# Sums of exponentials of the second row moved to PSUM, with new transfer widths

## Chip, cores, metric

One core of one Trainium2 chip. The metric is the device time of one execution, in microseconds; a kernel is run several times, and fast runs are compared with fast runs. (A run more than 1.5% above the fastest of its kernel would count as slow.)

## The reference

```python
batch, num_classes = 256, 32000            # logits float32, labels int32, smoothing 0.1
log_probs = logits - max(logits)           # per row
log_probs = log_probs - log(sum(exp(log_probs)))
smooth_targets[i, :] = smoothing / num_classes      # at the label: + 1 - smoothing
return -sum(smooth_targets * log_probs, axis=-1)
```

So each row needs two sums over 32,000 columns, one of the logits and one of their exponentials, the logit at the label, and one logarithm (Ln). The input is 32.77 MB and is read once.

## The kernel before

Each of the 128 partitions holds two rows. The first row comes in three transfers, the second in eleven that get shorter. For every transfer VectorE (DVE) sums the logits and ScalarE (ACT) takes exponentials (the exponentials themselves go to a "junk" tile that nobody reads; only their sum counts); each instruction writes its sum with a second, small one that reads the engine's accumulator ("READ_ACCUMULATOR": 0.187 us a piece on ScalarE and 0.08 on VectorE where it writes SBUF, in the profile of before).

```python
WIDTHS = (
    (8000, 12480, 11520),
    (8192, 6336, 4608, 3392, 2496, 1920, 1472, 1152, 960, 768, 704),
)
TURN_MAX = 4608
...
turn = ctx.enter_context(tc.tile_pool(name="turn", bufs=2))
...
esum = small.tile([P, len(WIDTHS[-1])], FP32, name="esum", tag="esum")   # SBUF
...
def sum_exps(xt, w, out):
    if w > TURN_MAX:
        ja = junk.tile([P, max(WIDTHS[0])], BF16, name="ja", tag="ja")
    else:
        ja = turn.tile([P, TURN_MAX], BF16, name="jt", tag="jt")
    return nc.scalar.activation(out=ja[:, :w], in_=xt[:, :w], func=AF.Exp, accum_out=out)
...
elast = psum.tile([P, 1], FP32, name="elast", tag="elast")
pairs = [small.tile([P, 2], FP32, ...) for i in range(2)]                # SBUF
for t, w in enumerate(WIDTHS[r]):          # left = transfers still to come
    part = sum_logits(xt, w, xsum[:, t + 1 : t + 2] if left > 1 else pairs[1 - left][:, 0:1])
    if left == 0:    exps = sum_exps(xt, w, elast[:])
    elif left <= 2:  exps = sum_exps(xt, w, pairs[2 - left][:, 1:2])
    else:            exps = sum_exps(xt, w, esum[:, t : t + 1])
    ...
    # left == 2: reduce xsum and esum into done[0]; left == 1, 0: done[i+1] = done[i] + pairs[i]
...
nc.scalar.activation(out=lse[:], in_=elast[:], func=AF.Ln, bias=done[2][:, 1:2])
```

The softmax here doesn't subtract the row's maximum and nothing guards it: scores larger than these inputs give would overflow.

## Time and profile before

| | before |
|---|---|
| time, median of 3 runs | 84.26 us (84.2 to 84.3) |
| span of the profile | 82.4 us |
| ScalarE busy, VectorE busy | 70%, 45% |
| mean HBM rate over the span | 398 GB/s |
| last transfer lands (estimate in the prediction) | 78.53 us |
| Ln starts | 79.50 us |

How to read it: neither engine is busy all the time, the transfers are (DMA share 0.97 to 1.09 in each of five windows that cover 1 to 78 us). What can be gained lies between the last landing and Ln; the prediction shows the lines.

### The profile page before, as it was taken

What the parts mean: (1) busy time and instruction counts of PE and PEld (TensorE: products, weight loads), DVE (VectorE), ACT (ScalarE), POOL (GpSimd) and SP (SyncE); (2) the same over time, 40 slices, a digit from 0 to 9 for tenths busy, and PEclk for the clock granted to TensorE, in tenths of its full rate; (3) what the DMA queues carried; (4) which work ended last, traced back from release to release, by engine and by line L of the source; (5) the groups of instructions that cost most, each with busy time, mean ns of one, the idle gap of its engine ahead of it and who ended that gap; (6) DMA issues with size and microseconds to landing.
All of it is one profiled execution on the core that took longest, in us unless ns stands there. A gap on an engine that the chain in (4) does not pass through costs nothing.

```text
span 82.4 us, 227 instructions
## 1 busy us (share of the span) xinstructions
PE 6.9 (8%) x21; PEld 4.9 (6%) x21; DVE 36.9 (45%) x35; ACT 58.1 (70%) x31; POOL 9.7 (12%) x19
## 2 busy tenths in 40 slices
PE   0000000000000000000000000000100000999020
PEld 0000000000000000000000000000000000886000
DVE  0000002980000999300399606950695845757760
ACT  5000002999100999992399999999999999999960
POOL 3201640030100000000000004970000000000000
PEclk9999999999999999999999999999999999999995
DMA  6999999999998889988969969998999999999800
GB/s 131 387 428 420 419 591 388 388 388 436 630 484 358 358 358 402 671 358 358 461 302 509 509 267 517 455 394 376 429 429 430 421 428 425 420 420 411 348 0 0
DMA packets 2258, 32.77 MB, mean 398 GB/s; under 512 B 337, under 2 KB 338, under 8 KB 1106
## 3 DMA queue, kind: packets, MB, share of 16 engines
q1 hardware_dynamic: 2018, 30.71, 87.8%
q10 hardware_dynamic: 144, 2.06, 5.9%
q0 software_dynamic: 96, 0.00, 0.1%
HBM read 32.77 MB, written 0.00 MB: 398 GB/s over the span
## 4 chain that ended last, share of the span: by engine, by line
DMA 48%; ACT 47%; issue 1%; SPq 0%; PE 0%; DVE 0%; ACTq 0%
DMA wide<-in_logits_dram 48%; ACT ja L209 27%; ACT jt L209 19%; SPq L188 0%; PE lse_t L216 0%; DVE res L315 0%; ACT lse L310 0%; ACT lse L250 0%; ACTq L209 0%
## 5 line engine op out<-in xcount | busy, mean ns | idle before, releaser
L209 ACT ACTIVATE ja<-wide 128x8000 bf16<-128x8000 f32 (+4 forms) x5 | 39.8, 7958 | 20.7 <-DMA wide<-in_logits_dram 20.7
L194 DVE SCALAR_TENSOR_TENSOR jd<-wide 128x4000 f32<-128x4000 f32 (+11 forms) x12 | 34.4, 2870 | 38.9 <-DMA wide<-in_logits_dram 38.9
L209 ACT ACTIVATE jt<-wide 128x4608 bf16<-128x4608 f32 (+6 forms) x7 | 14.6, 2093 | 0.0
L301 PE MATMUL warm<-wide,ident 128*128 128x256 f32 x18 | 6.0, 508 | 11.6 <-DMA wide<-in_logits_dram 11.6
L236 POOL TENSOR_TENSOR acc<-acc,sums 128x2 f32<-128x2 f32 x1 | 4.1, 4127 | 12.6 <-ACT ja L209 12.6
L301 PEld LDWEIGHTS warm<-wide,ident 128*128 128x128 f32 x18 | 4.7, 267 | 12.8 <-DMA wide<-in_logits_dram 11.9
L216 PE MATMUL loss_t<-ident,loss 128*1 128x128 f32 x1 | 0.4, 373 | 58.1 <-POOL loss L252 58.1
L216 PEld LDWEIGHTS loss_t<-ident,loss 128*1 128x1 f32 x1 | 0.1, 79 | 58.1 <-POOL loss L252 58.1
L236 POOL TENSOR_TENSOR acc<-sums 128x2 f32<-128x2 f32 x1 | 0.2, 192 | 16.2 <-ACT ja L209 16.2
L132 POOL DMA_INDIRECT gat<-in_logits_dram,flat_idx x2 | 2.0, 994 | 0.7 <-POOL ident masks.py:199 0.4
L255 DVE COPY res<-loss_t 1x128 f32<-1x128 f32 x1 | 0.3, 280 | 3.8 <-PE loss_t L216 3.8
L99 ACT ACT_TABLE_LOAD x1 | 1.3, 1283 | 0.9 <-PEq L342 0.9
L209 ACT ACTIVATE jt<-tail 128x768 bf16<-128x768 f32 (+1 forms) x2 | 1.6, 800 | 0.0
L153 POOL TENSOR_SCALAR weighted<-gat 128x1 f32<-128x1 f32 x1 | 0.8, 812 | 6.4 <-DMA gat<-in_logits_dram,flat_idx 6.4
L209 ACT ACTIVATION_READ_ACCUMULATOR jt<-wide 128x1 f32 x7 | 1.3, 187 | 0.0
L194 DVE SCALAR_TENSOR_TENSOR jd<-tail 128x384 f32<-128x384 f32 (+1 forms) x2 | 1.1, 542 | 0.0
L194 DVE DVE_READ_ACCUMULATOR jd<-wide 128x1 f32 x12 | 1.0, 81 | 0.0
L209 ACT ACTIVATION_READ_ACCUMULATOR ja<-wide 128x1 f32 x5 | 0.9, 187 | 0.0
L112 POOL DMA_DIRECT2D lab<-in_labels_dram x1 | 0.8, 766 | 1.0 <-POOLq L342 1.0
L124 POOL TENSOR_TENSOR flat_idx<-rowoff,lab 128x2 int32<-128x2 int32 x1 | 0.2, 193 | 5.3 <-DMA lab<-in_labels_dram 5.3
L153 POOL TENSOR_SCALAR xsum<-gat 128x1 f32<-128x1 f32 x1 | 0.2, 208 | 2.9 <-DMA gat<-in_logits_dram,flat_idx 2.9
L216 PE MATMUL lin_t<-ident,done 128*1 128x128 f32 x1 | 0.3, 270 | 3.3 <-DVE done L294 3.3
(22 smaller groups left out, 4.3 us busy)
## 6 DMA issues: line engine op xcount, KB each, us to landing
wide<-in_logits_dram SPq DMA_DIRECT2D x1, 6240.0 KB, 26.0
wide<-in_logits_dram SPq DMA_DIRECT2D x1, 5760.0 KB, 39.2
wide<-in_logits_dram SPq DMA_DIRECT2D x1, 4096.0 KB, 29.2
wide<-in_logits_dram SPq DMA_DIRECT2D x1, 3168.0 KB, 19.9
wide<-in_logits_dram SPq DMA_DIRECT2D x1, 2304.0 KB, 25.0
wide<-in_logits_dram ACTq DMA_DIRECT2D x1, 2016.0 KB, 13.8
wide<-in_logits_dram SPq DMA_DIRECT2D x1, 1984.0 KB, 11.4
wide<-in_logits_dram SPq DMA_DIRECT2D x1, 1696.0 KB
```

The source lines that it names most:

```text
L99: nc.scalar.add_instruction(mybir.InstLoadActFuncSet(name=nc.get_next_instruction_name(), act_func_set_id=tbl, ins=[], outs=[],))
L112: nc.gpsimd.dma_start(out=lab[:], in_=labels.bitcast(I32).rearrange("(p f) -> p f", p=P))
L124: nc.gpsimd.tensor_tensor(out=flat_idx[:], in0=rowoff[:], in1=lab[:].rearrange("p (r two) -> p r two", two=2)[:, :, 0:1], op=ALU.add,)
L132: nc.gpsimd.indirect_dma_start(out=gat[:, r : r + 1], out_offset=None, in_=logits[:], in_offset=bass.IndirectOffsetOnAxis(ap=flat_idx[:, r ...
L153: nc.gpsimd.tensor_scalar(out=weighted[r], in0=gat[:, r : r + 1], scalar1=label_weight, scalar2=None, op0=ALU.mult,)
L194: return nc.vector.scalar_tensor_tensor(out=jd[:, :h], in0=xt[:, :h], scalar=1.0, in1=xt[:, h:w], op0=ALU.mult, op1=ALU.add, accum_out=out,)
L209: return nc.scalar.activation(out=ja[:, :w], in_=xt[:, :w], func=AF.Exp, accum_out=out)
L216: nc.tensor.transpose(out=row[:], in_=column, identity=ident[:])
L236: nc.gpsimd.tensor_tensor(out=acc[:], in0=total, in1=sums[:, :, t : t + 1], op=ALU.add)
L255: nc.vector.tensor_copy(out=res[:, :, 0:1], in_=loss_t[:])
L301: nc.tensor.matmul(warm[:], lhsT=ident[:], rhs=xt[:, i * WARM_COLS : (i + 1) * WARM_COLS], start=True, stop=True,)
```

## The change

The intent: in the profile of before ScalarE's one accumulator read to PSUM took 0.149 us, those to SBUF 0.187 us, so eight sums go to a PSUM tile (esum) and two to the PSUM tiles pair0 and pair1; with cheaper steps the widths can shrink towards a shorter last transfer (576 instead of 704 columns).

```diff
-    (8192, 6336, 4608, 3392, 2496, 1920, 1472, 1152, 960, 768, 704),
+    (8640, 6400, 4608, 3392, 2496, 1856, 1408, 1088, 832, 704, 576),
...
-    esum = small.tile([P, len(WIDTHS[-1])], FP32, name="esum", tag="esum")
+    esum = psum.tile([P, len(WIDTHS[-1]) - 3], FP32, name="esum", tag="esum")
...
-        small.tile([P, 2], FP32, name=f"pair{i}", tag=f"pair{i}") for i in range(2)
+        psum.tile([P, 2], FP32, name=f"pair{i}", tag=f"pair{i}") for i in range(2)
```

## The prediction

> **What bounds the kernel now.** I read the page first, then the chain of waits in order of time, then the timelines of ScalarE (ACT) and VectorE (DVE) near the end, then the windows of the last microseconds.
>
> The page's slices show the transfers busy to slice 37 and nothing after:
>
> ```profile
> ACT  5000002999100999992399999999999999999960
> DMA  6999999999998889988969969998999999999800
> ```
>
> The chain in order of time names transfers up to 40.46 us and ScalarE from there to the end:
>
> ```profile
> 1.29 39.17 DMA wide<-in_logits_dram
> ...
> 76.73 0.98 ACT jt L209 x2
> 77.71 0.01 issue
> 77.72 0.85 ACT jt L209 x2
> 78.57 0.07 issue
> 78.64 0.84 ACT jt L209 x2
> 79.47 0.02 issue
> 79.50 0.27 ACT lse L310
> ```
>
> That looks like a ScalarE bound, but the VectorE timeline corrects it. These rows are start, length, instruction, and in brackets the idle time before it with what ended it:
>
> ```profile
> 63.15 2.56 DVE L194 SCALAR_TENSOR_TENSOR jd<-wide 128x2304 f32<-128x2304 f32 x1 [1.01 <-DMA wide<-in_logits_dram]
> ...
> 76.78 0.66 DVE L194 SCALAR_TENSOR_TENSOR jd<-wide 128x480 f32<-128x480 f32 x1 [0.41 <-DMA wide<-in_logits_dram]
> ...
> 78.55 0.52 DVE L194 SCALAR_TENSOR_TENSOR jd<-tail 128x352 f32<-128x352 f32 x1
> 79.00 0.08 DVE L194 DVE_READ_ACCUMULATOR jd<-tail 128x1 f32 x1
> 79.19 0.16 DVE L294 TENSOR_TENSOR done<-done,pair 128x2 f32<-128x2 f32 x1
> ```
>
> VectorE waits for each transfer and starts at its landing; ScalarE starts the same transfer at most 0.12 us later (63.17 and 76.82 for these two). So the stream sets the pace and the widths were already shaped so that ScalarE finishes one transfer as the next lands. The starts of 4608 columns (63.15) and of 768 columns (77.69, also VectorE's) are 12,160 columns apart: 14.54 us / 12,160 = 1.196 ns a column, against 0.833 ns a column on ScalarE. In the windows, the DMA share is 0.97 in 77.5 to 78.0 us and 0.07 in the next half microsecond. The last landing, estimated, is 77.69 + 704 x 1.196 ns = 78.53 us. No split of the same bytes moves that, while the stream has no hole. **What can be won is only what lies between 78.53 and 79.50 us**, where Ln starts; from Ln on (transpose, add, output transfer) nothing changes.
>
> The ScalarE rows of the end:
>
> ```profile
> 77.81 0.83 ACT L209 ACTIVATE jt<-tail 128x768 bf16<-128x768 f32 x1
> 78.54 0.19 ACT L209 ACTIVATION_READ_ACCUMULATOR jt<-tail 128x1 f32 x1
> 78.64 0.77 ACT L209 ACTIVATE jt<-tail 128x704 bf16<-128x704 f32 x1
> 79.31 0.15 ACT L209 ACTIVATION_READ_ACCUMULATOR jt<-tail 128x1 f32 x1
> 79.50 0.26 ACT L310 ACTIVATE lse<-elast,done 128x1 f32<-128x1 f32 x1
> ```
>
> The read of the accumulator takes 0.187 us on average (the groups' mean) where it writes SBUF, and 0.149 us in the one case where its target, elast, is in PSUM. From the start of 768 columns to that of 704 it is 0.83 us, 0.64 of columns and 0.19 of fixed cost: 0.093 from ACTIVATE and 0.094 from the read.
>
> [...] 827 ns at 768 columns is 640 + 187, and the read starts 0.10 before the ACTIVATE's end. [...] The trace agrees for latency, 149 against 187 ns; it does not show whether the next instruction also starts earlier, since Ln had to wait for elast. [...]
>
> **The change, part by part.** *Ten of the second row's eleven sums go to PSUM* (eight in esum, two in the pairs; the last was there). If the overlap stays 93 ns, the read costs ScalarE 149 - 93 = 56 ns instead of 94, so a transfer costs 0.149 instead of 0.187 us beyond its columns. This is worth 0.38 us of ScalarE time over ten, but ScalarE waits for the stream, so most turns into idle time, not into an earlier end.
>
> *The widths.* Arrivals, counted back from 78.53 at 1.196 ns a column: 576 at 78.53, 704 at 77.84, 832 at 77.00, 1088 at 76.00, 1408 at 74.70, 1856 at 73.02, 2496 at 70.80, 3392 at 67.81, 4608 at 63.76, 6400 at 58.24, 8640 at 50.59. ScalarE takes each at its arrival + 0.04, or when free. From 2496, at 70.84: 70.84 + 2.080 + 0.149 = 73.07 (1856), + 1.547 + 0.149 = 74.77 (1408), + 1.322 = 76.09 (1088), + 1.056 = 77.15 (832), + 0.842 = 77.99 (704), + 0.736 = 78.73 (576). Then 0.480 + 0.093 to the last read, 79.30, and 0.19 to Ln as now: **79.49, against 79.50**. The last transfer is 128 columns (0.107 us) shorter but starts 0.09 later than the last one now, because the smaller steps leave ScalarE a small backlog. Without the PSUM saving the same sum from 3392 on with 0.187 gives a last start of 78.97 and Ln at 79.73.
>
> *The pairs in PSUM.* Column 0 of each is written by VectorE, column 1 by ScalarE for the transfer before. In SBUF these had nothing to do with each other. [...] I expect VectorE's sum of the last but one transfer to wait until ScalarE has finished the transfer before it, and likewise for the last. The path then is: ScalarE's 832 starts 77.15, its read ends at 77.15 + 0.693 + 0.093 + 0.149 = 78.09; VectorE starts the 704 at 78.12; its read 0.45 later as in the rows above (79.00 - 78.55), the add 0.19 later at 78.76, the next sum 0.18 later at 78.94; for 288 columns a side 0.45 - 64/960 = 0.38 to the read, 79.32, add at 79.51, end 79.67, and 0.05 to whoever waits (79.35 to TensorE's 79.40 now): **Ln at 79.72, 0.22 us later than now**. Without the wait, VectorE starts the 832 at 77.00, the two reductions cost 0.33 as now, 704 starts about 77.84, the last add ends at 79.39, and Ln is ScalarE's again at 79.49. Ln needs both engines, so the larger counts.
>
> **The rivals.** *Saving without wait*: Ln at 79.49, 84.25 us. For it: the program runs VectorE and ScalarE in near lockstep, and the wait might already be over. Against: before, VectorE's last sum starts at 78.55, before ScalarE's previous read has ended (78.73). *Saving and wait*: +0.22, 84.48 us; VectorE becomes the bound at the very end. *No saving in issue, only in latency*: +0.23 without the wait (84.5), +0.44 with it (84.7); for it speaks that the next ACTIVATE may be bound by issue, not by the end of the read. *Everything better than I count*: if the read to PSUM hides wholly, ScalarE takes each transfer at arrival, the last at 78.57, and Ln comes at 78.57 + 0.573 + 0.19 = 79.33, -0.17, 84.1 us. *The transfers move*: larger rows of 8640 columns, or a hole in the stream since the first buffer is awaited; nothing in the DMA slices speaks for it, as 8640 is issued after the same release as 8192.
>
> **Range and chances.** I give the saving 0.8 and a wait that binds 0.45, and so: saving alone 0.44 x -0.01, both 0.36 x 0.22, wait alone 0.09 x 0.44, neither 0.11 x 0.23; the sum is +0.14. The widths were chosen by someone who measured, which speaks for the lower side, so I shade it to +0.04: 84.3 us. The range takes in -0.26 (all hidden, and a little of the stream's spread: the three runs differ by 0.1) to +0.3 (both engines' costs). Two per cent is 1.69 us, more than the whole 0.97 us between last landing and Ln; faster by that is impossible unless the stream changes, slower needs a hole in it. Faster 0.01, within 0.98, slower 0.01.
>
> **What would show it.** The ten reads near 149 ns instead of 187, and the time from read start to next ACTIVATE 0.056 instead of 0.094: the saving. VectorE's starts on 832, 1088 and 1408 columns at about 77.00, 76.00, 74.70: the stream is unmoved. The wait: VectorE's rows for 352 and 288 columns starting just after ScalarE's reads, with idle time put down to ScalarE. ScalarE's last ACTIVATE at 78.7, and Ln after VectorE's last add or after the last read tells which engine ends it. I would be wrong if ScalarE shows gaps growing to the end (a larger saving), if the last landing is not near 78.5, or if VectorE's reads from PSUM take longer than the 156 to 161 ns of the reductions and adds now.

The forecast's sum: 0.44 x -0.01 + 0.36 x 0.22 + 0.09 x 0.44 + 0.11 x 0.23 = +0.14 us, shaded to +0.04, which on 84.25 us gives the 84.3. The constants are from the rows of before. ScalarE's 0.833 ns a column is (4027 - 774) ns / (4608 - 704) columns; the 93 ns of overlap are the read's 187 ns less 94 from its start to the next ACTIVATE (0.09 or 0.10 in the rows); 64/960 us is 64 columns at VectorE's rate, (6659 - 524) ns / (6240 - 352) columns = 1.042 ns. That no split moves the last landing was an estimate; after's 832 columns landed at 76.89 us where it gave 77.00.

## The result and the profile after

85.31 us median (85.12 to 85.45, 4 runs) against 84.25 us (4 runs): 1.06 us slower, ratio 1.0121, 95% interval 1.0103 to 1.0139. (Ratios and intervals are from fast runs alone; they are not quite the ratios of the medians quoted.) That is outside the predicted range of 84.0 to 84.6. The profiled run of after was the fastest of its four, 85.12 us with a span of 83.3 us, so its trace shows 0.9 of the 1.06 us.

The slices of after first:

```profile
ACT  5000003999001999990599998999999999999960
DMA  5999998899888899888996999999999999999300
```

The transfers still end in slice 37. In the windows the share of the DMA engines is 0.68 in 77.5 to 78.0 us and 0.01 in the next half microsecond, where before had 0.97 and 0.07: the stream is not what got longer. ScalarE's timeline of after (start us, length us, instruction), in the middle and at the end of the second row:

```profile
67.77 0.15 ACT L209 ACTIVATION_READ_ACCUMULATOR jt<-wide 128x1 f32 x1
67.96 3.03 ACT L209 ACTIVATE jt<-wide 128x3392 bf16<-128x3392 f32 x1
70.89 0.15 ACT L209 ACTIVATION_READ_ACCUMULATOR jt<-wide 128x1 f32 x1
71.08 2.29 ACT L209 ACTIVATE jt<-wide 128x2496 bf16<-128x2496 f32 x1
...
77.78 0.15 ACT L209 ACTIVATION_READ_ACCUMULATOR jt<-wide 128x1 f32 x1
77.83 0.89 ACT L209 ACTIVATE jt<-wide 128x832 bf16<-128x832 f32 x1
78.62 0.16 ACT L209 ACTIVATION_READ_ACCUMULATOR jt<-wide 128x1 f32 x1
78.67 0.79 ACT L209 ACTIVATE jt<-tail 128x704 bf16<-128x704 f32 x1
79.35 0.17 ACT L209 ACTIVATION_READ_ACCUMULATOR jt<-tail 128x1 f32 x1
79.40 0.69 ACT L209 ACTIVATE jt<-tail 128x576 bf16<-128x576 f32 x1
79.97 0.18 ACT L209 ACTIVATION_READ_ACCUMULATOR jt<-tail 128x1 f32 x1
80.36 0.26 ACT L310 ACTIVATE lse<-elast,done 128x1 f32<-128x1 f32 x1 [0.21 <-DVE done L294]
```

Two kinds of step are to be seen. The reads are short, as hoped: 0.15 us in the middle. But at 67.77 and 70.89 the next ACTIVATE comes **0.19 us** after the start of the read, when the read has ended; at 77.78, 78.62 and 79.35 it comes **0.05 us** after it. Before, it was 0.09 or 0.10 us between these steps. At one place before had 0.22 us: the read at 50.25 is followed by an ACTIVATE at 50.47, though its columns had landed by 50.22, where VectorE starts on them. In the compiled program that ACTIVATE waits for the one before it, as the junk tile of the long transfers has one buffer. So the price of such a wait stood in the trace of before. The last ACTIVATE starts at 79.40 instead of 78.64.

VectorE's timeline of after, near the end:

```profile
76.89 0.59 DVE L194 SCALAR_TENSOR_TENSOR jd<-wide 128x416 f32<-128x416 f32 x1 [0.28 <-DMA wide<-in_logits_dram]
...
77.97 0.17 DVE L289 TENSOR_REDUCE done<-esum 128x1 f32<-128x8 f32 x1 [0.47 <-ACT jt L209]
...
78.81 0.53 DVE L194 SCALAR_TENSOR_TENSOR jd<-tail 128x352 f32<-128x352 f32 x1 [0.60 <-ACT jt L209]
79.26 0.14 DVE L194 DVE_READ_ACCUMULATOR jd<-tail 128x1 f32 x1
...
80.11 0.16 DVE L294 TENSOR_TENSOR done<-done,pair 128x2 f32<-128x2 f32 x1
```

The 832 columns land at 76.89 us (predicted 77.00), so the stream is in place. VectorE then sits idle for ScalarE twice, which no row of before shows: for the sums in esum, and before the sum of the 704 columns, which starts at 78.81, just after ScalarE's read for 832 columns has ended at 78.78. Its last add ends at 80.27, and Ln waits 0.21 us for it.

Where the 0.19 us come from can be read in the compiled program. The fourth second-row ACTIVATE of each kernel, with what it waits on (the DMA queues, and "Activation", ScalarE's own count of finished instructions):

```
before  L209 Activation jt,esum<-wide 128x3392 [waits DMAHW7]
after   L209 Activation jt,esum<-wide 128x3392 [waits DMAHW7,Activation]
```

I read off the count of that wait for each ACTIVATE. Before, from 2496 columns on, each waits for the last but one (because the junk output has two buffers), which has long ended: the 1920 columns start at 72.47, and the read for 3392, on which they wait, was over at 70.30. After, the ACTIVATEs of 4608, 3392, 2496, 1856, 1408 and 1088 columns wait for the one immediately before them; 832, 704 and 576 do not. The six are just those that write esum right after another write to esum (the 6400 has the first row's Ln between, and waits for the 8640).

### The profile page after: what moved, and what is told of

The parts are those of the page before. It is cut to its first block, busy times and chain, and to the rows that moved or that the text cites. A ratio compares the mean times of both kernels' runs of the same rounds, so it can differ in the third digit from the quotient of the medians.

```text
span 83.3 us, 228 instructions
## 1 busy us (share of the span) xinstructions
PE 7.4 (9%) x21; PEld 5.2 (6%) x21; DVE 37.0 (44%) x35; ACT 58.4 (70%) x31; POOL 10.3 (12%) x19
## 4 chain that ended last, share of the span: by engine, by line
DMA 52%; ACT 40%; issue 4%; DVE 2%; PE 0%; ACTq 0%; DVEq 0%
DMA wide<-in_logits_dram 52%; ACT ja L209 24%; ACT jt L209 16%; DVE jd L194 1%; DVE lin_row L313 0%; PE lin_t L216 0%; DVE res L315 0%; DVE done L294 0%; ACT lse L250 0%; ACTq L209 0%; DVEq L315 0%
## 5 line engine op out<-in xcount | busy, mean ns | idle before, releaser
L301 PE MATMUL warm<-wide,ident 128*128 128x256 f32 x18 | 6.5, 540 | 11.6 <-DMA wide<-in_logits_dram 11.6
L241 POOL TENSOR_TENSOR lin<-acc,weighted 128x1 f32<-128x1 f32 x1 | 4.6, 4604 | 0.1
L236 POOL TENSOR_TENSOR acc<-acc,sums 128x2 f32<-128x2 f32 x1 | 0.2, 195 | 12.6 <-ACT ja L209 12.6
L209 ACT ACTIVATE jt<-tail 128x704 bf16<-128x704 f32 (+1 forms) x2 | 1.4, 739 | 0.0
L194 DVE SCALAR_TENSOR_TENSOR jd<-tail 128x352 f32<-128x352 f32 (+1 forms) x2 | 1.0, 491 | 0.6 <-ACT jt L209 0.6
```

Of the source, the lines that this page charges most:

```text
L194: return nc.vector.scalar_tensor_tensor(out=jd[:, :h], in0=xt[:, :h], scalar=1.0, in1=xt[:, h:w], op0=ALU.mult, op1=ALU.add, accum_out=out,)
L236: nc.gpsimd.tensor_tensor(out=acc[:], in0=total, in1=sums[:, :, t : t + 1], op=ALU.add)
L241: nc.gpsimd.tensor_tensor(out=lin[:], in0=total[:, 0, :], in1=weighted[0], op=ALU.add)
L301: nc.tensor.matmul(warm[:], lhsT=ident[:], rhs=xt[:, i * WARM_COLS : (i + 1) * WARM_COLS], start=True, stop=True,)
```

## The experiments

My theory after the result ("bank" stands here for a stretch of PSUM on which the program put writes one after the other: a small PSUM tile of after, esum or a pair, or one half, 512 columns, of the 1024-column tile tried below, whose two halves did not wait for each other): **the change puts eight sums of one engine into one PSUM bank, and for every write after a write in that bank the program waits for the one before to end; this, six times, is most of the loss. The rest is VectorE's wait for the bank of the pairs.** (The table below adds a third, smaller part, the widths.) Rival A: the widths cost it (a first transfer of 8640 columns for which ScalarE waits 0.29 us, and shorter steps). Rival B: the pairs carry it. Rival C: writing to PSUM is slow in itself.

The first four ran on one chip, beside the kernel before at 84.40 us median (84.24 to 84.79, 11 runs). All eleven runs gave correct results.

### New widths alone

Edit: only the first line of the change.

> The new widths alone, all sums in SBUF. My theory (waits): nothing waits that did not before; ScalarE pays 0.187 us beyond the columns at each transfer, so it runs behind the stream by a little more at each of the short ones; last ACTIVATE near 78.95, Ln near 79.7, 0.2 us more than the kernel before (84.45 us). Rival A (the widths are the cost: smaller steps and a first transfer of 8640 that lands after ScalarE is free): most of the 1.06 us appears here, 85.1 us or more.

Measured 84.44 us (84.38 to 84.52), ratio 1.000 (0.9983 to 1.0018). In the profile the last ACTIVATE starts at 78.89 and Ln at 79.64, as expected. By the trace the widths cost 0.14 us (Ln was at 79.50 before), or 0.24 if one allows for a stream that was 0.1 us earlier (the third transfer starts ScalarE at 40.44, before at 40.54); the times show nothing. Rival A falls as the main cause.

### esum in one bank, pairs in SBUF

```diff
 # new widths, and
+    esum = psum.tile([P, len(WIDTHS[-1]) - 3], FP32, name="esum", tag="esum")
 # pairs stay in small (SBUF)
```

> New widths, esum in PSUM as in the change, the pairs left in SBUF. Theory: the six ACTIVATEs of 4608 to 1088 columns still start 0.18 to 0.19 us after the read before them (it must have ended), so ScalarE is as late as in the changed kernel at 1088; VectorE's last two sums no longer wait, Ln follows the last read. 0.1 to 0.2 us less than the changed kernel, about 85.15 us. Rival A: same as the widths alone. Rival B (the pairs' waits are the cost): close to 84.4 us.

Measured 85.33 us (84.96 to 85.65), ratio 1.0096 (1.0066 to 1.0125). The loss is there without the pairs, so rival B falls. How much of it is not to be read from this median: the expected 0.1 to 0.2 us under the changed kernel does not show, because three runs took 84.96 to 85.17 us and three 85.49 to 85.65. In the profiled run (85.63 us) the whole stream was 0.6 us late, its third transfer starting ScalarE at 41.05 us where after's trace has 40.44; of the other two long runs there is no trace. Within the trace such a delay drops out. The two starts on which the table below rests:

```profile
58.83 5.54 ACT L209 ACTIVATE ja<-wide 128x6400 bf16<-128x6400 f32 x1
...
78.47 0.89 ACT L209 ACTIVATE jt<-wide 128x832 bf16<-128x832 f32 x1
```

### esum in two banks by turns

```diff
-    esum = psum.tile([P, len(WIDTHS[-1]) - 3], ...)
+    esum = psum.tile([P, 1024], ...)                  # t even: first half, odd: second half
...
-            exps = sum_exps(xt, w, esum[:, t : t + 1])
+            at = t % 2 * 512 + t // 2
+            exps = sum_exps(xt, w, esum[:, at : at + 1])
...
-    in_=esum[:, :t], axis=AX.X
+    in_=esum[:].rearrange("p (b c) -> p b c", b=2)[:, :, : t // 2], axis=AX.XY
```

> As the one before, but esum spans two PSUM banks and the sums go to them by turns, so that each ACTIVATE waits only for the one before the last. Theory (the wait is the cost, not PSUM): reads still 0.15 us, next ACTIVATE 0.05 to 0.06 us after the read's start instead of 0.19; last ACTIVATE near 78.8, Ln near 79.55, 84.3 us, within 0.1 us of the kernel before. Rival C (writing sums to PSUM is slow in itself): no better than with one bank, about 85.15 us.

Measured 84.26 us (84.15 to 84.42), ratio 0.9976 (0.9958 to 0.9995). ScalarE's timeline of this kernel:

```profile
58.42 5.54 ACT L209 ACTIVATE ja<-wide 128x6400 bf16<-128x6400 f32 x1
...
74.79 0.16 ACT L209 ACTIVATION_READ_ACCUMULATOR jt<-wide 128x1 f32 x1
74.84 1.37 ACT L209 ACTIVATE jt<-wide 128x1408 bf16<-128x1408 f32 x1
76.11 0.16 ACT L209 ACTIVATION_READ_ACCUMULATOR jt<-wide 128x1 f32 x1
76.16 1.11 ACT L209 ACTIVATE jt<-wide 128x1088 bf16<-128x1088 f32 x1
...
77.22 0.90 ACT L209 ACTIVATE jt<-wide 128x832 bf16<-128x832 f32 x1
```

As many writes to PSUM as with one bank, the same number of instructions, and the ACTIVATEs of the six steps start 0.05 us after the read's start (once 0.08). In the compiled program their wait is for the last but one again. The loss is gone; rival C falls.

### The wait without PSUM

```diff
 # the kernel before, and
-    turn = ctx.enter_context(tc.tile_pool(name="turn", bufs=2))
+    turn = ctx.enter_context(tc.tile_pool(name="turn", bufs=1))
```

> The kernel before, nothing in PSUM that was not there, old widths; only the junk output of the short ACTIVATEs has one buffer instead of two, so that eight of them (3392 to 704 columns) must wait for the one before to end. Theory: next ACTIVATE 0.22 us after the start of the read of 0.187 us, instead of 0.094; eight times 0.128 us, so ScalarE ends about 1.0 us later, 85.2 us. Rival C: 84.25 us, as nothing is written to PSUM.

Measured 85.40 us (85.36 to 85.48), ratio 1.0115 (1.0097 to 1.0133): 1.0 us, as expected. Its ScalarE timeline:

```profile
70.26 0.19 ACT L209 ACTIVATION_READ_ACCUMULATOR jt<-wide 128x1 f32 x1
70.48 2.29 ACT L209 ACTIVATE jt<-wide 128x2496 bf16<-128x2496 f32 x1
72.67 0.19 ACT L209 ACTIVATION_READ_ACCUMULATOR jt<-wide 128x1 f32 x1
72.89 1.81 ACT L209 ACTIVATE jt<-wide 128x1920 bf16<-128x1920 f32 x1
```

0.22 us from read to ACTIVATE. The same kind of wait, made by a single junk buffer in SBUF, gives a loss with nothing moved to PSUM. The total is like that of the change by chance, as there are eight such waits here and six there; the price of one agrees: from the start of 4608 columns to that of 704 it is 79.76 - 63.17 = 16.59 us against 78.64 - 63.17 = 15.47 before, 0.14 for each of eight, and one bank against two gives 0.84 us for six (table below), again 0.14. With the two-bank kernel this settles that the wait is the cost.

### PSUM with the old widths, and the pairs

The next four ran on one chip beside the kernel before at 84.30 us median (84.13 to 84.79, 11 runs). First the two PSUM edits with the widths of before:

> Both PSUM edits of the change, the widths of before. Theory (six waits of ScalarE on itself plus the two of VectorE): six steps with 0.28 us fixed instead of 0.187, less two steps with 0.15, so ScalarE about 0.5 us later, and VectorE's last sums 0.2 us more: 0.7 us over the kernel before, about 85.1 us. Rival A (widths): 84.3 to 84.4 us, as before.

Measured 85.00 us (84.89 to 85.21), ratio 1.0082 (1.0055 to 1.0108): 0.70 us, as expected. Most of the loss does not need the new widths.

Second, the two-bank kernel with the pairs in PSUM (edit: the third part of the change, and lin_t and loss_t in one bank):

> The kernel with esum in two banks, and now the pairs in PSUM too, each written by both engines. (The two transposed rows lin and loss share a bank[...].) This is the state that the prediction called saving and wait. Theory: VectorE's sum of 704 columns starts just after ScalarE's read for 832, near 78.2, the last add near 79.5, Ln near 79.75 and released by VectorE: 0.1 to 0.2 us over the two-bank kernel. Rival: the pairs cost nothing, as VectorE has time: the same as the two-bank kernel, or 0.08 us less.

Measured 84.44 us (84.31 to 84.61), ratio 1.0014 (0.9988 to 1.0041). VectorE's and ScalarE's rows, in this order:

```profile
78.19 0.53 DVE L194 SCALAR_TENSOR_TENSOR jd<-tail 128x352 f32<-128x352 f32 x1 [0.16 <-ACT jt L209]
...
79.49 0.16 DVE L298 TENSOR_TENSOR done<-done,pair 128x2 f32<-128x2 f32 x1
...
79.74 0.26 ACT L314 ACTIVATE lse<-elast,done 128x1 f32<-128x1 f32 x1 [0.21 <-DVE done L298]
```

This is the prediction's case "saving and wait", and its row is met: predicted 78.12 for the start, 79.51 for the last add, 79.72 for Ln. That it is met to 0.02 us is in part luck: the stretch from 6400 columns to Ln took 21.34 us where 21.44 was predicted, and began 0.12 us later. What was expected of this run, 0.1 to 0.2 us over the two-bank kernel, agrees with the trace (Ln at 79.74 against 79.64) and with the medians (84.44 here; 84.26 and, in a repeat below, 84.27), but the intervals of the ratios overlap.

Third, new widths and the pairs in PSUM with esum in SBUF:

> New widths and the pairs in PSUM, esum in SBUF. Theory: no wait of ScalarE on itself, so no large loss; VectorE's two waits make Ln about 0.1 us later than with the widths alone, near 79.75, 0.1 us over the widths alone. Rival B (the pairs carry the change's cost): 0.5 us or more over the kernel before.

Measured 84.56 us (84.50 to 84.63), ratio 1.0029 (1.0004 to 1.0053), 0.12 us over the widths alone (other job; by the traces 0.11, Ln at 79.75 against 79.64). The pairs cost about a tenth of a microsecond, not one.

### A version meant to beat both

```diff
 # the two-bank kernel, and (in words)
-    pairs: SBUF [P, 2], VectorE's and ScalarE's sum together
+    pairs: PSUM [P, 1] each, ScalarE's sum alone (lin_t and loss_t share a bank)
-    done[i + 1][P, 2] = done[i] + pairs[i]
+    done[i + 1][P, 1] = done[i] + pairs[i]
-    reduce xsum before the last two transfers; last two sums of logits go to the pairs
+    all sums of logits to xsum in SBUF, one reduction after the last
```

> A version that should beat both: esum in two PSUM banks by turns, the two last but one sums of exponentials each alone in a PSUM bank, all of VectorE's sums in SBUF (one reduction at the end in place of one earlier and two halves of adds), new widths. No bank is written by two engines, none twice running by ScalarE. Theory: every step of ScalarE costs 0.15 us, two more than in the two-bank kernel by 0.04 us each; Ln near 79.5, 0.08 us less than the two-bank kernel, 0.2 to 0.3 us less than the kernel before. Rival: ScalarE waits for landings there, and nothing is won over the two-bank kernel.

Measured 84.47 us (84.33 to 84.59), ratio 1.0016 (0.9991 to 1.0042). A miss: Ln at 79.39 is the earliest of all traces so far, but the time did not follow; the profiled run has 2.1 us between span and time where the others have about 1.8. A last job of three, beside the kernel before at 84.27 us median (84.11 to 84.79, 12 runs, of which 11 are those of the job before), asked again:

> The split kernel once more. Its profile had the earliest Ln of all (79.39) but its times were 0.17 us over the kernel before, with 2.1 us between span and time where the others have 1.8. If the 2.1 us was chance of that round: 84.1 to 84.2 us. If it belongs to the kernel: again about 84.45 us and again 2.1 us beside the span.

Measured 84.43 us (84.13 to 84.69), ratio 1.0016 (0.9990 to 1.0043). The profiled run, 84.13 us with a span of 82.4, has 1.7 us beside the span, but the other five have 2.0 to 2.2, and all six of the first job 1.9 to 2.2. Every run of every other kernel has 1.7 to 1.9. So the extra 0.2 to 0.3 us goes with this kernel, in eleven of twelve runs, and takes back whatever it gains inside the span. What it is I cannot explain, and the version is not shown to be faster.

> The two-bank kernel with the new widths once more, to see whether its small gain holds. If it holds: 0.1 to 0.3 us less than the kernel before. If it was scatter: equal to it within 0.1 us.

Measured 84.27 us (84.13 to 84.44), ratio 0.9991 (0.9965 to 1.0018). The small gain of the first job did not hold.

> esum in two banks by turns, the widths of before, pairs in SBUF. Theory: ScalarE's steps of 0.15 us are shorter than the landings are apart at these widths, so ScalarE waits for landings and the saving turns into idle time; the last ACTIVATE (704) starts at its landing, near 78.6, and Ln is near 79.5 as before: within 0.1 us of the kernel before. Rival (the two banks alone gain, the widths are beside the point): 0.2 us less than before, as the new widths with two banks.

Measured 84.26 us (84.14 to 84.40), ratio 0.9994 (0.9968 to 1.0019), as the theory has it. From ScalarE's timeline:

```profile
63.06 4.03 ACT L209 ACTIVATE jt<-wide 128x4608 bf16<-128x4608 f32 x1
...
72.23 0.16 ACT L209 ACTIVATION_READ_ACCUMULATOR jt<-wide 128x1 f32 x1
72.39 1.80 ACT L209 ACTIVATE jt<-wide 128x1920 bf16<-128x1920 f32 x1
...
78.53 0.79 ACT L209 ACTIVATE jt<-tail 128x704 bf16<-128x704 f32 x1
```

and VectorE's row for the same 1920 columns:

```profile
72.40 1.16 DVE L194 SCALAR_TENSOR_TENSOR jd<-wide 128x960 f32<-128x960 f32 x1 [0.88 <-DMA wide<-in_logits_dram]
```

The ACTIVATE of 1920 columns comes 0.16 us after the read's start, not 0.05: both engines begin when the columns land. At 960 columns it is the same (76.69, VectorE at 76.70). From 4608 to 704 columns it is 78.53 - 63.06 = 15.47 us, exactly as before (78.64 - 63.17): what PSUM saves is spent waiting for landings. With the repeat counted, none of the versions without added waits is told apart from the kernel before.

### The two costs side by side

From the ScalarE timelines, for the kernels with the new widths. The first column of numbers is the time from the start of the 6400-column ACTIVATE to that of the 832-column one (seven steps that write esum; in the kernels with one bank six of them end in a wait); the second from there to Ln. Differences within a trace do not depend on how late the stream was as a whole. The repeats of the two-bank kernel and of the split kernel have 18.74 and 18.75 us in the first column, 2.45 and 2.38 in the second, so a difference under 0.1 us is near the scatter.

| kernel | 6400 to 832, us | 832 to Ln, us |
|---|---|---|
| predicted, saving and pairs' wait | 18.87 | 2.57 |
| after | 77.83 - 58.19 = 19.64 | 80.36 - 77.83 = 2.53 |
| esum in one bank | 78.47 - 58.83 = 19.64 | 80.88 - 78.47 = 2.41 |
| widths alone (SBUF) | 77.24 - 58.21 = 19.03 | 79.64 - 77.24 = 2.40 |
| pairs in PSUM, esum in SBUF | 77.24 - 58.21 = 19.03 | 79.75 - 77.24 = 2.51 |
| two banks | 77.22 - 58.42 = 18.80 | 79.64 - 77.22 = 2.42 |
| two banks, pairs in PSUM | 77.20 - 58.40 = 18.80 | 79.74 - 77.20 = 2.54 |
| split | 77.03 - 58.24 = 18.79 | 79.39 - 77.03 = 2.36 |

One bank for esum costs 0.84 us against two, and 0.61 against SBUF, with the pairs in either place. Pairs in PSUM cost 0.11 to 0.12 us, wherever esum is. With the widths these make up the whole: between the traces of before and after Ln moved by 80.36 - 79.50 = 0.86 us, of which the widths are 0.14 (79.64 - 79.50), the one bank 0.61 and the pairs 0.11 to 0.12. The three traces after, widths alone and before differ by at most 0.1 us in when the stream came.

## Why the prediction was wrong

- **What bounds it.** Right: the landings of after were 0.1 to 0.2 us before the predicted ones, and no version without the waits got under the kernel before in a way that a repeat upheld. The estimated last landing, 78.53, rests on a start (77.69) at which VectorE had only just become free, but the split kernel supports it: VectorE waits there for the last two landings too and starts at 76.95, 77.87 and 78.58 on the last three transfers; 1.196 ns a column would give 77.79 and 78.48 after 76.95. That the result lies within two per cent, given a chance of 0.98, came true too.
- **"A transfer costs 0.149 instead of 0.187 us beyond its columns."** This step failed, for six of the ten. From start to start less 0.833 ns a column: the step of 2496 columns took 72.47 - 70.21 - 2.08 = 0.18 us before, 73.45 - 71.08 - 2.08 = 0.29 us after and 73.15 - 70.91 - 2.08 = 0.16 us with two banks. What failed in it is "if the overlap stays 93 ns": in these six steps the next ACTIVATE began 0.19 us after the read's start, with no overlap left, and not 0.056. From 6400 to 832 columns ScalarE took 19.64 - 18.87 = 0.77 us more than predicted, and that put the last ACTIVATE at 79.40 instead of 78.73. The part about the engine was right: where no wait was added, the next ACTIVATE came 0.05 us after the read's start (0.056 predicted), and the two-bank kernel has 18.80 us where 18.87 was predicted. What the prediction missed is a wait of ScalarE on itself. It expected writes of two engines in one bank to be put one after the other, and looked for the place only in the pairs, where two engines meet; that eight writes of a single engine share the bank of esum, and are put one after the other too, it did not ask.
- **"ScalarE waits for the stream, so most turns into idle time."** Right for a saving with the old widths (15.47 us with and without it). With the new ones the saving came through, 19.03 - 18.80 = 0.23 us, and went to pay for the widths. The sentence hid the other side: ScalarE had nearly no slack at each landing, so the six added waits came through to the end. In after ScalarE starts 0.17 us behind VectorE on the 4608 columns (63.82 against 63.65), 0.46 on the 2496 (71.08 against 70.62) and 0.94 on the 832 (77.83 against 76.89); in before it was never more than 0.12 from 4608 on.
- **"The pairs in PSUM."** Right in mechanism and in place: VectorE started the 704 columns just after ScalarE's read (78.81 after 78.78), and Ln was VectorE's. The 0.22 us of the prediction were against the kernel before, and the two-bank kernel with pairs has the predicted Ln (79.74, predicted 79.72; in part luck, as said). The 0.12 us of the table are against pairs in SBUF, which pay 0.04 us more for each of two reads (0.09 us from read to next ACTIVATE, 78.01 to 78.10 and 78.78 to 78.87 in the two-bank kernel, against 0.05). Against the split kernel, which has the cheap reads and no such wait, the wait costs 2.54 - 2.36 = 0.18 us; the prediction has 2.57 - 2.34 = 0.23 for the same. What it named as a possible surprise, longer reads of PSUM by VectorE, hardly showed in the length of an instruction: the reduction of eight sums took 0.156 us from SBUF and 0.166 from PSUM, the two adds 0.161 and 0.156 on average. VectorE's accumulator read, of which it said nothing, took 0.082 us to SBUF and 0.140 to PSUM (means of the last two transfers, before and after).
- **The widths.** The sum without saving and without wait gave Ln at 79.73, 0.23 us later than before; the trace of the widths alone has 79.64, in a stream 0.1 us earlier. In the time the difference did not show (84.44 against 84.40).
- **The range.** Its largest loss was the rival "no saving in issue, only in latency" with the pairs' wait, +0.44 us; a case in which a transfer costs more than before was not among the rivals. Nothing in the profile spoke for the shade to the low side; its ground was that whoever chose the widths had measured. "Slower needs a hole in it" overlooks the same thing: this loss, though under two per cent, came without a hole in the stream.

Left open: whether the chip needs the wait between two writes of one engine to one bank. The program has it, and no run here took it away within a bank.

## What to carry to other kernels

When an operand moves from SBUF to PSUM, ask what the move does to the list of waits, not only to the instruction: here neighbours in one bank were put in order though they touch different columns and belong to one engine, six times at 0.14 us. Two banks by turns for sums written one after the other took the 0.84 us away again, and two engines writing halves of one small tile cost 0.11 to 0.12 us. And where an engine runs in step with a stream, a saving in it can be worth nothing, as with the old widths here (15.47 us with and without it), while the six added waits counted in full (with the new widths 0.61 us of the 0.86 by which Ln moved, over sums in SBUF).
